# Decoder layer on one core: a fifth seven-product pair in the second feed-forward, and block sums made in the activation pool

## The chip, the cores and the metric

The kernel runs on one core of one Trainium2 chip. The metric is the time of one execution on the device, in microseconds (us), as the median of three runs. The engines are named as in the profile: PE multiplies matrices (PEld is its loading of stationary operands), DVE is VectorE, ACT is ScalarE, POOL is GpSimd, and SP is the queue that issues most loads.

## The reference

One decoder layer, in float32, for a sequence of 256 tokens of width 2048 with 16 learned tokens put ahead of it (272 rows in all):

```
s = concat(meta, x)
s = s + 0.5 * ffn(rms_norm(s), ffn1)             # silu(h Wg) * (h Wu), then Wd; inner width 5632
h = rms_norm(s)
q, k, v, b, c, u = split(h @ w_in)
y_att  = differential attention (8 heads, 2 softmaxes each, difference times lam), head norm
y_conv = b * shortconv(c * u)                    # 3 taps
s = s + (sum over both branches of sigmoid(h @ w_gate) * (y @ w_branch)) @ w_out
s = s + 0.5 * ffn(rms_norm(s), ffn2)
out = rms_norm(s)[16:]
```

The second feed-forward only has to be computed for the 256 real tokens. Its gate and up weights are 2048 x 11264, its down weights 5632 x 2048.

## The kernel before

**Products in two parts.** Every float32 operand is split into a high half, rounded for PE, and the rest, a low half. A product is the sum of three matmuls: high by high, low by high, high by low. For weights, ACT casts the loaded tile into `wh` (`cast`, line 503) and DVE subtracts to make `wl` (`rest`, line 506). There are three buffers of each (`W_BUFS`), and a buffer comes free when PE has read it last. Loaded weight tiles of 128 x 1024 lie in the tag `st`, with eight buffers (`raw_tile`, line 68).

**Stages.** The first feed-forward runs in two halves of its inner width with `linear` (line 311), in blocks of two chunks of weights; after each block it calls `store.tick()`. Then come the projections with attention and convolution between their blocks, the gates and branches (`Mixed`, line 510), the output projection (`Plain`, line 685), and the second feed-forward: three thirds of the inner width, of four, four and three gate-up linears, each third followed by two down linears, all of class `Mixed`.

**Direct and seven-product pairs.** `Mixed` treats two chunks of the contraction (256 rows) as a pair, with two halves of the tokens and two column groups of 512. A pair is thus a 2 x 2 by 2 x 2 product of blocks. A direct pair (kind D, line 565) does the eight block products, 24 matmuls of 128 x 512, in two slots. A seven-product pair (kind S, line 594) does seven, 21 matmuls, in four slots: `raw` (P1, C11), `sums` (P5, P7), `sums2` (P6, C21) and `single` (C12). It needs sums of weight blocks, `ta` (two blocks) and `tb` (two blocks), and sums of activation blocks. The sums of weights come from one of two places. Where `store.get` finds them, they are loaded from memory (lines 609, 626); elsewhere DVE makes them in four additions (lines 614, 615, 623, 624). The last down linear, u = 1 of the last third, takes every pair directly.

**The store.** The sums in memory are made early, from the raw weights, by `Store.tick` (line 281). Every `STEP` ticks a unit begins: it loads two tiles `ur` and `un` on SP; half a step later four additions on DVE make `ua` and `ub`, and POOL writes both to memory. All four tiles are `st` buffers. `store.want` lists the units in the order in which they are made, all but the third S pair of each linear.

**The order of the work.** `stream` (line 664) calls, for each slot n, the preparation of slot n + 2, the products of slot n, the steps placed after it, and then as many entries of the list `todo` as the slot's `room` says: two after the slots of a direct pair, none after those of a seven-product pair. `todo` holds DVE's combining of results (`Gated.late`, `Added.late`) and of the turned activations (`Pairs.turned`, placed after slots 4 and 5). DVE's operations in this part form a chain: they run in the order written. PE and ACT have no such chain; the scheduler that builds the program may put a later instruction of theirs ahead of one that would wait.

**Kinds and pools.** `HALF` gives the kinds of the eight pairs of the gate-up linears, `TURNED` with `ORDER` those of the down linears of the first two thirds, `SHORT` those of the last. An activation pair of kind D takes one slot of the pool `act` (`N_ACT` slots), one of kind S two. Small results lie in the tag `ev`, with eight buffers.

## Time and profile before

| | |
|---|---|
| median of three runs | 2189.27 us (2188.91 to 2189.32) |
| profiled execution, its own time | 2188.72 us |
| span of that execution, first to last instruction | 2186.9 us |
| granted clock of PE | 0.999 |
| PE busy | 2173.7 us, 99% of the span |
| DVE busy | 1643.5 us, 75% |
| ACT busy | 1109.3 us, 51% |
| moved by DMA | 542.09 MB, 248 GB/s on average |

The span is what the trace covers; the run's own time has 1.8 us around it. In the trace a line such as "L84 DVE TENSOR_TENSOR wl<-st,wh 128x1024" names the code line (a helper's, where one records every operation, as line 84 does for DVE and line 560 for PE), the engine, the operation, the tile written and the tiles read. A value in square brackets is the engine's idle time before the instruction, with what ended it. In rows of busy time by windows, each engine's busy us is followed by its number of instructions; the last three columns are the granted clock, the mean share of the DMA engines that were busy, and GB/s. The first feed-forward takes about the first 815 us, the projections with attention and convolution go to 1130, the gates and branches to 1388, the output projection to 1483, and the second feed-forward takes the rest.

### The profile page before, as it was taken

The numbers are of one execution on the slowest core, as the hardware profiler recorded it, in microseconds if no ns is written. First come the engines' busy times: TensorE is split into PE (matmuls) and PEld (weight loads), VectorE is DVE, ScalarE is ACT, GpSimd is POOL, SyncE is SP. The second block draws the span as 40 slices with busy tenths as digits, with TensorE's granted clock in tenths as the row PEclk, the third lists the DMA queues.
The fourth block names the chain that finished last, engine by engine and source line by source line (L and its number), as shares of the span: only waits on it lengthen the run. The fifth ranks groups of instructions, "written<-read, shape, count | busy, mean of one in ns | idle before, by whom it ended". The sixth has DMA issues, their size and how long they took to land.

```text
span 2186.9 us, 34858 instructions
## 1 busy us (share of the span) xinstructions
PE 2173.7 (99%) x13450; PEld 1955.7 (89%) x13450; DVE 1643.5 (75%) x2214; ACT 1109.3 (51%) x1431; POOL 60.6 (3%) x119
## 2 busy tenths in 40 slices
PE   9999999999999999999999999999999999999998
PEld 8999999999999999999988888888878888888886
DVE  7767665566766767666777787768888988888888
ACT  6434333333433444444445555556666566655665
POOL 0000000000000000000000000000000000000000
PEclk9999999999999999999999999999999999999999
DMA  7787888879888988744556665656777877878874
GB/s 238 263 309 275 294 295 288 301 261 317 302 276 287 320 294 303 260 145 135 167 162 212 212 207 190 211 180 216 250 239 258 280 238 259 273 244 277 282 244 154
DMA packets 240966, 542.09 MB, mean 248 GB/s; under 512 B 18564, under 2 KB 18624, under 8 KB 240800
## 3 DMA queue, kind: packets, MB, share of 16 engines
q1 hardware_dynamic: 225184, 484.25, 66.5%
q0 software_dynamic: 15232, 54.96, 6.7%
q8 instruction: 105, 1.72, 0.3%
q10 hardware_dynamic: 384, 0.66, 0.1%
q14 instruction: 61, 0.50, 0.1%
HBM read 486.18 MB, written 53.61 MB: 247 GB/s over the span
## 4 chain that ended last, share of the span: by engine, by line
PE 98%; ACT 1%; DVE 1%; DMA 1%; issue 0%; DVEq 0%
PE pgC L560 12%; PE pdC L560 7%; PE pgP L560 6%; PE gC L560 5%; PE pd L346 4%; PE pu L346 4%; PE pu L344 4%; PE pd L344 4%; PE pu L345 4%; PE pd L345 4%; PE pg L346 4%; PE pg L344 4%; PE pg L345 4%; PE zC L560 3%; PE o L709 3%; PE pgD L560 3%
## 5 line engine op out<-in xcount | busy, mean ns | idle before, releaser
L331 ACT CAST wh<-st 128x1024 fp32r<-128x1024 f32 x352 | 369.6, 1051 | 566.9 <-PE pd L345 134.8
L332 DVE TENSOR_TENSOR wl<-st,wh 128x1024 fp32r<-128x1024 f32 x352 | 429.6, 1222 | 273.8 <-ACT wh L331 273.2
L84 DVE TENSOR_TENSOR wl<-st,wh 128x1024 fp32r<-128x1024 f32 x246 | 299.3, 1220 | 85.2 <-ACT wh L504 78.2
L504 ACT CAST wh<-st 128x1024 fp32r<-128x1024 f32 x238 | 247.4, 1053 | 184.2 <-PE o L709 39.9
L344 PE MATMUL pg<-h,wh 128*128 128x272 f32 x704 | 202.8, 289 | 1.7 <-ACT wh L84 1.4
L344 PE MATMUL pu<-h,wh 128*128 128x272 f32 x704 | 203.2, 289 | 0.0
L346 PE MATMUL pd<-m,wl 128*128 128x272 f32 x704 | 203.0, 288 | 0.0
L346 PE MATMUL pu<-h,wl 128*128 128x272 f32 x704 | 203.0, 288 | 0.0
L344 PE MATMUL pd<-m,wh 128*128 128x272 f32 x704 | 203.0, 288 | 0.0
L345 PE MATMUL pu<-h,wh 128*128 128x272 f32 x704 | 202.4, 288 | 0.0
L345 PE MATMUL pd<-m,wh 128*128 128x272 f32 x704 | 202.4, 287 | 0.0
L345 PE MATMUL pg<-h,wh 128*128 128x272 f32 x704 | 201.4, 287 | 0.0
L346 PE MATMUL pg<-h,wl 128*128 128x272 f32 x704 | 199.7, 289 | 0.0
L560 PE MATMUL pgC<-wh,h 128*128 128x512 f32 x528 | 163.3, 391 | 0.0
L344 PEld LDWEIGHTS pg<-h,wh 128*128 128x128 f32 x704 | 132.3, 188 | 2.6 <-ACT wh L84 2.6
L504 ACT CAST wh<-ta 128x1024 fp32r<-128x1024 f32 x74 | 77.9, 1052 | 108.3 <-DVE ta L84 72.7
L345 PEld LDWEIGHTS pg<-h,wh 128*128 128x128 f32 x704 | 132.8, 189 | 0.0
L345 PEld LDWEIGHTS pu<-h,wh 128*128 128x128 f32 x704 | 132.7, 189 | 0.0
L345 PEld LDWEIGHTS pd<-m,wh 128*128 128x128 f32 x704 | 132.7, 189 | 0.0
L346 PEld LDWEIGHTS pu<-h,wl 128*128 128x128 f32 x704 | 132.5, 188 | 0.0
L346 PEld LDWEIGHTS pd<-m,wl 128*128 128x128 f32 x704 | 132.5, 188 | 0.0
L344 PEld LDWEIGHTS pu<-h,wh 128*128 128x128 f32 x704 | 132.2, 188 | 0.1
(479 smaller groups left out, 5162.0 us busy)
## 6 DMA issues: line engine op xcount, KB each, us to landing
st<-in_ffn_w_gu_dram SPq DMA_DIRECT2D x176, 512.0 KB, 5.9
st<-in_ffn_w_down_dram SPq DMA_DIRECT2D x140, 512.0 KB, 6.2
st<-in_w_in_dram SPq DMA_DIRECT2D x96, 512.0 KB, 4.4
st<-in_ffn_w_gu_dram SPq DMA_DIRECT2D x176, 256.0 KB, 4.3
sr<-in_ffn_w_gu_dram SPq DMA_DIRECT2D x44, 512.0 KB, 4.2
st<-in_w_gate_dram SPq DMA_DIRECT2D x40, 512.0 KB, 4.7
ur<-in_ffn_w_gu_dram SPq DMA_DIRECT2D x33, 512.0 KB, 7.8
un<-in_ffn_w_gu_dram SPq DMA_DIRECT2D x33, 512.0 KB, 5.0
```

What stands on the lines that cost most here:

```text
L84: r = f(*a, **k)
L331: act_.copy(out=wh[:, :m, :], in_=sw)
L332: dve_.tensor_sub(wl[:, :m, :], sw, wh[:, :m, :].bitcast(F32))
L344: nc.tensor.matmul(a, wh[:, i, f], act.part(c, 0, t0, t1), start=first, stop=False)
L345: nc.tensor.matmul(a, wh[:, i, f], act.part(c, 1, t0, t1), start=False, stop=False)
L346: nc.tensor.matmul(a, wl[:, i, f], act.part(c, 0, t0, t1), start=False, stop=last)
L504: nc.scalar.copy(out=wt[0][:, : sw.shape[1], :], in_=sw)
L560: nc.tensor.matmul(ps[:, f0:f1], x, wt[:, f0:f1], start=count[n] == self.whole[n], stop=count[n] == 1)
L709: nc.tensor.matmul(a, wh[:, i, f], act.both(c, 0, SEQ), start=first, stop=False)
```

## The change

The kinds get a fifth S pair (`FIVE` for `HALF`, and `TURNED`, with its order) and the last third's down linear a third one (`SHORT`). In the new order all S pairs of a linear stand together behind the direct ones. In linears with five S pairs the third one still makes its own sums; where there are fewer than five, all are loaded. The store's list grows from 47 to 63 units. Until the end of the first feed-forward a unit begins every five ticks, its four tiles are slots of the activation pool, and its additions are divided over two ticks; from the projections on it goes on with six ticks and `st` buffers. The activation pool gets two slots more, and small tiles (constants of the start, norms, attention) move into `ev` buffers. Slots of S pairs with loaded sums have room for one entry of `todo`.

```diff
-N_ACT = 28
+N_ACT = 30
...
-HALF = "DDDSSDSS"
-TURNED = "DSDSDSDS"
-ORDER = (0, 2, 4, 1, 3, 6, 5, 7)
-SHORT = "DDDSDS"
-STEP = 6
+FIVE = "DDDSSSSS"
+TURNED = "DSDSDSSS"
+ORDER = (0, 2, 4, 1, 3, 5, 6, 7)
+SHORT = "DDDSSS"
+STEP = 5
...
-    grow = const.tile([DC, P], F32, name="grow")
+    grow = ev([DC, P], "grow")
...
-                self.ssq = tmp.tile([P, T], F32, tag="ssq", name="ssq")
-            sq = self.ssq if first else tmp.tile([P, T], F32, tag="sq", name="sq")
+                self.ssq = ev([P, T], "ssq")
+            sq = self.ssq if first else ev([P, T], "sq")
...
+        def tile(self, name):
+            if self.step == STEP:
+                return apool.tile([P, 2, GW], F32, tag="act", name=name)
+            return raw_tile(name)
+
         def tick(self):
-            n = self.count % STEP
+            n = self.count % self.step
...
-                self.v = [raw_tile(n) for n in ("ur", "un")]
+                self.v = [self.tile(n) for n in ("ur", "un")]
...
-            if n == STEP // 2 and self.v:
+            if n == 3 and self.v:
+                r, x = self.v
+                ta = self.tile("ua")
+                self.v.append(ta)
+                nc.vector.tensor_add(ta[:, 0, :], r[:, 0, :], x[:, 0, :])
+                nc.vector.tensor_add(ta[:, 1, :], x[:, 1, :], x[:, 0, :])
+                nc.gpsimd.dma_start(out=self.units[0][-1][0], in_=ta.rearrange("p c f -> p (c f)"))
+            if n == 4 and self.v:
                 kept = self.units.pop(0)[-1]
-                (r, x), self.v = self.v, None
-                ta, tb = raw_tile("ua"), raw_tile("ub")
-                added(nc.vector, r, x, ta, tb)
-                for tl, to in zip((ta, tb), kept):
-                    nc.gpsimd.dma_start(out=to, in_=tl.rearrange("p c f -> p (c f)"))
...
+                (r, x, ta), self.v = self.v, None
+                tb = self.tile("ub")
+                nc.vector.tensor_add(tb[:, 0, :], ta[:, 0, :], x[:, 1, :])
+                nc.vector.tensor_add(tb[:, 1, :], tb[:, 0, :], r[:, 1, :])
+                nc.gpsimd.dma_start(out=kept[1], in_=tb.rearrange("p c f -> p (c f)"))
+
+        def slower(self):
+            assert self.v is None
+            self.step, self.count = STEP + 1, 0
...
+            room = 0 if kept is None else 1
...
-                Slot(raw, lambda: p((1, "P1", "r", 0), (2, "C11", "r", 1)), 0),
+                Slot(raw, lambda: p((1, "P1", "r", 0), (2, "C11", "r", 1)), room),
...
-    def in_store(kinds, order):
-        at = [g for g in order if kinds[g] == "S"]
-        return [g for n, g in enumerate(at) if n != 2]
+    def want(kinds, order, *place):
+        at = [k for k in order if kinds[k] == "S"]
+        for n, k in enumerate(at):
+            if n != 2 or len(at) < 5:
+                store.want(place[0], (place[1] + 2 * k) * P, *place[2:])
...
+    while store.v:
+        store.tick()
+    store.slower()
     for g in range(2):
         linear(h2, allk, w_in, 0, W2 + g * GW, 0, T, "k", qk_evict(kT, g, 0, "k"))
...
-    h3 = Pairs("h3", HALF)
+    h3 = Pairs("h3", FIVE)
```

More of the change, by code (lines that the diff above doesn't have):

```diff
@@ L123, in decoder_layer @@
     NV = 2 * DC + 3 * NH + 1
-    vrows = const.tile([NV, P], F32, name="vrows")
+    vrows = ev([NV, P], "vrows")
     G_MIX, G_FFN2, G_CONV, G_SUB = 0, DC, 2 * DC, NV - 1
@@ L135, in decoder_layer @@
     nc.gpsimd.dma_start(out=vrows[G_SUB:NV, :], in_=t["subln"])
-    lamv = const.tile([P, 4, HD], F32, name="lamv")
+    lamv = ev([P, 4, HD], "lamv")
     for i, n in enumerate(("lambda_q1", "lambda_k1", "lambda_q2", "lambda_k2")):
@@ L171, in make_lam @@
     def make_lam():
-        lprod = tmp.tile([P, 2, HD], F32, tag="lprod", bufs=1, name="lprod")
+        lprod = ev([P, 2, HD], "lprod")
         nc.vector.tensor_mul(lprod, lamv[:, 0:4:2, :], lamv[:, 1:4:2, :])
@@ L237, in end @@
             nc.tensor.matmul(ps[:, n0:T], ones, self.ssq[:, n0:], start=True, stop=True)
-            ms = tmp.tile([P, T], F32, tag="ms", bufs=1, name="ms")
+            ms = ev([P, T], "ms")
             nc.vector.tensor_scalar(ms[:, n0:], ps[:, n0:T], 1.0 / D, EPS, op0=ALU.mult, op1=ALU.add)
@@ L255, in rsqrt @@
     def rsqrt(out_, ms, shape, name):
-        a = tmp.tile([P, T], F32, tag="rsa", bufs=1, name="rsa" + name)[:, : shape[1]]
+        a = ev([P, T], "rsa" + name)[:, : shape[1]]
         nc.scalar.activation(a, ms, AF.Sqrt)
@@ L270, in __init__ @@
         def __init__(self):
-            self.units, self.kept, self.count, self.v = [], {}, -DC // KB, None
+            self.units, self.kept, self.count, self.v, self.step = [], {}, -DC // KB, None, STEP
         def want(self, w, r0, c0, c1):
@@ L644, in mixed @@
             self.slots += [
-                Slot(raw, lambda: p((1, "P1", "r", 0), (2, "C11", "r", 1)), 0),
-                Slot(sums, lambda: p((5, "P5", "a", 0), (4, "P7", "a", 1)), 0),
-                Slot(sums2, lambda: p((6, "P6", "b", 0), (3, "C21", "b", 1)), 0),
-                Slot(single, lambda: p((7, "C12", "s", 0)), 0),
+                Slot(raw, lambda: p((1, "P1", "r", 0), (2, "C11", "r", 1)), room),
+                Slot(sums, lambda: p((5, "P5", "a", 0), (4, "P7", "a", 1)), room),
+                Slot(sums2, lambda: p((6, "P6", "b", 0), (3, "C21", "b", 1)), room),
+                Slot(single, lambda: p((7, "C12", "s", 0)), room),
             ]
@@ L975, in decoder_layer @@
         for g in third:
-            for k in in_store(HALF, range(8)):
-                store.want(w_gu, 2 * k * P, g * GW, F + g * GW)
+            want(FIVE, range(DC // 2), w_gu, 0, g * GW, F + g * GW)
         kinds, order = (TURNED, ORDER) if whole else (SHORT, range(6))
         for u in range(2 if whole else 1):
-            for k in in_store(kinds, order):
-                store.want(w_down, (third[0] * GC + 2 * k) * P, u * W2, u * W2 + GW)
+            want(kinds, order, w_down, third[0] * GC, u * W2, u * W2 + GW)
     before1 = First()
@@ L1117, in values @@
             nc.vector.tensor_copy(oN[g][:, qt, j, :], po[:, :P])
-            junk = tmp.tile([P, P], F32, tag="junk", bufs=1, name="junk")
+            junk = ev([P, P], "junk")
             nc.scalar.activation(junk, oN[g][:, qt, j, :], AF.Square, accum_out=osq[:, qt, h : h + 1])
@@ L1395, in decoder_layer @@
             turns = []
+    assert not store.units
     stream(linears)
```

5 lines of the change are left out of this document (removed).

## The prediction

> **What bounds the kernel now.** I read the page first, then the busy time in chosen windows, then the timelines of three engines over one gate-up linear of the second feed-forward.
>
> ```profile
> span 2186.9 us, 34858 instructions
> ...
> PE 2173.7 (99%) x13450; PEld 1955.7 (89%) x13450; DVE 1643.5 (75%) x2214; ACT 1109.3 (51%) x1431; POOL 60.6 (3%) x119
> ...
> DMA  7787888879888988744556665656777877878874
> ...
> PE 98%; ACT 1%; DVE 1%; DMA 1%; issue 0%; DVEq 0%
> ...
> L560 PE MATMUL pgC<-wh,h 128*128 128x512 f32 x528 | 163.3, 391 | 0.0
> ```
>
> PE sets the end nearly alone. But 391 ns is the life of one matmul, and matmuls overlap; what one saves is the distance between starts. The first gate-up linear of the second third shows it: 180 matmuls lie between these two rows.
>
> ```profile
> 1736.48 0.62 PE L560 MATMUL pgC<-wh,h 128*128 128x512 f32 x2
> ...
> 1777.34 0.61 PE L560 MATMUL pgC<-wh,h 128*128 128x512 f32 x2
> ```
>
> 40.86 / 180 = 0.227 us each. The next rows cut a later linear (first third) into its stretches: three direct pairs, two seven-product pairs, one direct pair, two seven-product pairs; then three other places.
>
> ```profile
> 1567.56:1585.54 17.98, 17.98 (x85) 14.80 (x84) 16.11 (x20) 9.40 (x12) 0.00 (x0) 1.00 0.83 280
> 1585.54:1595.56 10.02, 10.02 (x46) 7.70 (x44) 8.12 (x11) 8.39 (x11) 0.00 (x0) 1.00 0.54 162
> 1601.02:1610.77 9.75, 9.75 (x43) 7.75 (x42) 8.15 (x9) 7.80 (x10) 0.00 (x0) 1.00 0.81 257
> 1567.56:1610.77 43.21, 43.21 (x193) 34.75 (x192) 37.80 (x46) 27.70 (x34) 0.00 (x0) 1.00 0.76 253
> ...
> 1610.00:1617.00 7.00, 7.00 (x33) 5.77 (x32) 6.88 (x10) 3.91 (x5) 0.00 (x0) 1.00 1.04 395
> ...
> 68.00:309.00 241.00, 241.00 (x1922) 241.00 (x1921) 164.35 (x223) 96.27 (x110) 13.82 (x26) 1.00 0.85 292
> ...
> 972.00:1130.00 158.00, 158.00 (x1159) 145.97 (x1158) 111.02 (x220) 72.39 (x136) 0.00 (x0) 1.00 0.51 156
> ```
>
> Two seven-product pairs are 42 matmuls, 9.52 us at 0.227; they take 10.02 and 9.75, so PE already loses 0.50 and 0.23 us there. The waits of the weight loads from 1480 us on name whom for:
>
> ```profile
> PEld pgP L560 <- DVE wl L84: 4.8, 15, 0.4
> PEld pgC L560 <- DVE wl L84: 2.1, 7, 0.3
> PEld pdP L560 <- DVE wl L84: 1.8, 6, 0.4
> PEld pdC L560 <- DVE wl L84: 0.9, 3, 0.3
> ```
>
> It is VectorE, late with the low half wl. So this stage has PE as its bound and DVE (37.80 of 43.21 us, 87%) just behind it, in runs of seven-product pairs above all.
>
> **What is taken away.** A direct pair is 24 matmuls, a seven-product pair 21. Eleven gate-up linears and five of the six down linears (the last stays all direct) turn one pair each: 16 x 3 = 48 matmuls, 48 x 0.227 = **10.9 us** off PE. By the means of the groups it would be 18.8; that would be an error.
>
> The Trainium skill (TensorE: Matmul & The Clock Gate, section "Wait — 56ns, not 53.3ns?") gives 215.7 ns between starts at 512 columns, which would make 10.4 us; its section "Back-to-back issue gap" has about 131 ns in a stream, which would make 6.3. The rows above agree with neither, and decide.
>
> **What the longer run costs.** Before, a linear goes D D D S S D S S; after, D D D S S S S S, 105 matmuls or 23.8 us in one run. Four of the five load their sums; the third (place 2) makes them itself, in four additions. Before, that pair stood behind a direct pair; now it stands behind two seven-product pairs. VectorE takes its work in the order written (a chain): rest of sr, two additions for ta, two for tb, rest of ta. The rows of VectorE and ScalarE for a self-made pair and for a loaded one behind another:
>
> ```profile
> 1596.99 1.22 DVE L84 TENSOR_TENSOR wl<-sr,wh 128x1024 fp32r<-128x1024 f32 x1
> 1598.12 0.68 DVE L84 TENSOR_TENSOR ta<-sr,sx 128x512 f32<-128x512 f32 x1
> 1598.72 0.68 DVE L84 TENSOR_TENSOR ta<-sx 128x512 f32<-128x512 f32 x1
> ...
> 1604.80 1.22 DVE L84 TENSOR_TENSOR wl<-sr,wh 128x1024 fp32r<-128x1024 f32 x1 [0.44 <-ACT wh L504]
> 1606.16 1.23 DVE L84 TENSOR_TENSOR wl<-ta,wh 128x1024 fp32r<-128x1024 f32 x1
> ```
> ```profile
> 1599.52 1.06 ACT L504 CAST wh<-ta 128x1024 fp32r<-128x1024 f32 x1 [2.90 <-DVE ta L84]
> ...
> 1603.71 1.06 ACT L504 CAST wh<-sr 128x1024 fp32r<-128x1024 f32 x1 [0.69 <-PE pgP L560]
> ```
> ```profile
> 1607.14 0.62 PE L560 MATMUL pgP<-wh,h3b 128*128 128x512 f32 x2
> ```
>
> Starts on DVE are 1.13 us apart behind a 1024-wide operation and 0.60 behind a 512-wide one. In a run the cast of sr cannot begin earlier than 1603.71: it waits for PE to give back one of three buffers. So a run leaves VectorE no lead, however early the data are. Put a self-made pair in the place of the loaded one: rest of sr from 1604.80, additions 1605.93 and 1606.53, ta there at 1607.21, cast done 1608.3. PE wants it at 1607.14: **1.2 us late**. Filling: PE may take the two first products of the last slot meanwhile, and the low half of ta is late behind the tb additions (1607.13 to 1608.33, rest done 1609.55, wanted 0.45 after the high half at 1608.75), 0.8 more. I take 1.25 a linear; bounds 0 (all filled) and 2.0.
>
> That holds where VectorE enters the run with nothing left over: first linears of the three thirds, second down linears of two, and the second gate-up of the last third, whose turned pairs are both direct: six. In the other linears the turned activations hold it up at the first pair:
>
> ```profile
> 1587.37 0.69 DVE L84 TENSOR_TENSOR ma<-xf,ma 128x512 fp32r<-128x512 f32 x1 [2.05 <-ACT ma L447]
> 1587.98 1.07 DVE L84 TENSOR_TENSOR xf<-xf 128x256 f32<-128x256 f32 x3
> 1588.97 1.22 DVE L84 TENSOR_TENSOR wl<-tb,wh 128x1024 fp32r<-128x1024 f32 x1
> ...
> 1594.72 2.35 DVE L84 TENSOR_TENSOR wl<-st,wh 128x1024 fp32r<-128x1024 f32 x2
> ```
>
> From 1588.97 it has no gap until the second pair is done at 1594.72, where now a direct pair gives it time (5.46 us of PE for two rests). After the change the next work there is the step the new pops bring forward (mb, 0.60), rest of sr (1.13), ta (1.28 to its landing), cast (1.1): 1598.8. PE, without loss, would want ta at 1585.54 + 0.09 (transposes) + 48 x 0.227 = 1596.5. Late by 2.3. Such a linear loses 0.5 today (0.09 of 0.50 is the transposes), some of which stays: **+2.0** each; bounds 0.1 (VectorE's work from 1588.97 to the run's last wl is 1.13 + 1.2 + 12.0 + 6.4 = 20.7, with 3 x 1.13 + 0.60 = 4.0 a loaded pair and 2.4 more a self-made one, ending 1609.7, PE's 1609.4, and no order of matmuls beats that) and 2.6. There are seven gate-up linears of this kind. The first down linears of two thirds now have two turned seven-product pairs ahead instead of one: one xf group and one 512 more, 0.99 + 0.60 on DVE, less what is hidden: +3.0 each (0.1 to 3.6). The down linear of the last third has a run of three, all loaded, behind such turns: +1.0 (-0.5 to 2).
>
> Sum: 6 x 1.25 + 7 x 2.0 + 2 x 3.0 + 1.0 = 28.5; less 10.9: **+17.6**. All low ends: -10.5; all high ends: +28.5.
>
> **What moves early on.**
>
> ```profile
> L303 DVE TENSOR_TENSOR ua<-un 128x512 f32<-128x512 f32 x47 | 32.2, 684 | 0.0
> ```
> ```profile
> SPq L325 <- DVE ub L304: 186.4, 46, 8.5
> ```
> ```profile
> sr<-in_ffn_w_gu_dram SPq DMA_DIRECT2D x44, 512.0 KB, 4.2
> ...
> sx<-in_ffn_w_gu_dram SPq DMA_DIRECT2D x33, 256.0 KB, 4.3
> ...
> ta<-sums0a SPq DMA_DIRECT2D x1, 512.0 KB, 3.2
> tb<-sums0b SPq DMA_DIRECT2D x1, 512.0 KB, 3.3
> ```
>
> 47 units become 63 (11 x 4 + 4 x 4 + 3). The first feed-forward gives 248 ticks of 241 / 80 = 3.01 us: 42 units at six ticks, 50 at five; the rest, 5 before and 13 after, go into the projections. A unit reads and writes 2.1 MB. Per tick 0.524 + 2.1/5 = 0.94 MB, 313 GB/s; the window shows 292 at a share of 0.85, so full is 343 and the share becomes 0.91. It stays under PE, and the weights have their eight buffers to themselves, where SP now waits 186 us for those the store holds: **0**. Its loads now wait on SP, ahead of weights, for a free activation slot; stream, h1 and m hold 4 + 8 + 12 = 24 of 30 and the store at most 5, and should one be late the eight weight buffers cover 24 us. If the bandwidth went, say 300 GB/s, a tick would take 3.14 us: +32. DVE gets 3.2 more units of four 0.60 us additions in those 241 us, beside 164: hidden. In the projections eight more units are 19 us on DVE, which is busy 111 of 158: hidden, at most 2. Constants and norms that go to the eight ev slots are used where PE has other work: 0.
>
> **The rivals.** (1) *The order hides it: faster.* PE's instructions aren't chained, and today it already runs later first-half products ahead of a late wl: the four waits above come to 9.6 us of weight loads, and cost 0.2 to 0.3 us a boundary. If that fills the new runs too, it is the low end: 2189.3 - 10.5 = **2178.8**. It decides where a linear loses less than 10.9 / 16 = 0.68 more. Against it: the late thing is here a high half, on which P5 and P7 whole hang. (2) *Even*: half of the stalls filled, 14 - 10.9: about 2192. (3) *Transfers set the run: slower still.* A loaded pair moves 1.84 MB, a self-made one 1.05; a run 8.4 MB in 23.8 us, 352 GB/s. By 253 / 0.76 = 333 it takes 25.2, +1.4 in 15 linears: 21 more, **2228**. Against it: the eight buffers hold 4 MB ahead, and one window had 395. (4) *The early stage is full*: +32, **2239**; against it the shares above.
>
> The Trainium skill (DMA: Bandwidth & Descriptors, section "Specifications") puts HBM at about 358 GB/s for a core, by which the run would have 6 GB/s to spare. The window of 395 GB/s is above that, so the trace doesn't agree.
>
> **How the numbers follow.** The sum stands against the profiled execution's own 2188.72 us (span 2186.9 and 1.8 around it): 2206.3. The median is 0.55 higher: **2206.9, say 2207**. Chances: forecast 0.60, (1) 0.17, (2) 0.10, (3) 0.08, (4) 0.05. A measurement here tells 0.2%, 4.4 us, from no change: faster is (1), 0.17; same (2), 0.10; slower the rest, 0.73. The range goes from 2183, which leaves out most of (1), to 2224, which holds the high ends (2218), 2 us of the projections and a part of (3). The forecast's own is 2194 to 2218.
>
> **What would show it.** Right: a clean gate-up linear takes 41.4 instead of 40.9 us, one with turns some 1.3 more than before; PE's losses stand at P5 of pair 5, "<- ACT wh" with "DVE ta" behind it; VectorE has no gap from the first pair to the fifth. Wrong: linears of 40.2 to 41.7 us, gaps on VectorE inside the run, a run whose idle times end on DMAs, or a matmul pitch over 3.01 us a tick in the first feed-forward.

## The result, and the profile after

The changed kernel takes 2270.9 us (median of four runs, 2268.4 to 2281.7) against 2189.2 before: a ratio of 1.038, 95% interval 1.035 to 1.042. The forecast was 2207, at most 2224. The sign was right, and the size was not: 82 us lost where 18 were expected.

The page of the changed kernel, its busy times, its DMA shares by slice, its chain and two groups of instructions:

```profile
span 2269.7 us, 35203 instructions
...
PE 2199.3 (97%) x13402; PEld 1955.3 (86%) x13402; DVE 1708.5 (75%) x2325; ACT 1141.2 (50%) x1474; POOL 77.9 (3%) x151
...
DMA  7888988977988988877666665557677778768874
...
PE 61%; issue 29%; DVE 5%; POOL 2%; ACT 1%; DMA 1%; POOLq 0%; DVEq 0%; SPq 0%; ACTq 0%
...
L356 PE MATMUL pd<-m,wl 128*128 128x272 f32 x704 | 205.8, 292 | 19.4 <-DVE wl L342 19.3
```

PE has 48 matmuls fewer (13402 for 13450), as the change says. The chain that ends last, 98% PE before, leaves PE for 39% of the span. In the first feed-forward PE now stands 19.3 us for VectorE's wl in the down products alone.

Where the time went is read from the first matmul of a stage. Before (timeline of PE):

```profile
815.42 0.29 PE L344 MATMUL k<-h,wh 128*128 128x272 f32 x1
...
1129.98 0.63 PE L560 MATMUL gC<-wh,h 128*128 128x512 f32 x2
...
1483.33 0.63 PE L560 MATMUL pgC<-wh,h 128*128 128x512 f32 x2
```

and after:

```profile
857.99 0.29 PE L354 MATMUL k<-h,wh 128*128 128x272 f32 x1
...
1176.16 0.63 PE L570 MATMUL gC<-wh,h 128*128 128x512 f32 x2
...
1529.41 0.63 PE L570 MATMUL pgC<-wh,h 128*128 128x512 f32 x2
```

The projections begin 42.6 us later, the gates 46.2, the second feed-forward 46.1. From there to the end of the span it was 703.6 us and is 740.3: 36.7 more. Two losses, then: **46 us early on**, where the prediction had 0, and **37 in the second feed-forward**, where it had 17.6.

**The early loss.** Which DMA VectorE waited for, and four windows of the first feed-forward (columns as in the prediction; the last three are granted clock, DMA share, GB/s):

```profile
DVE ua L302 <- DMA un<-in_ffn_w_gu_dram: 67.7, 20, 8.3
...
DVE ua L302 <- DMA un<-in_ffn_w_down_dram: 50.4, 12, 7.1
```
```profile
68.00:190.00 122.00, 121.72 (x968) 121.32 (x966) 81.40 (x112) 49.07 (x55) 8.58 (x16) 1.00 0.89 303
319.00:487.00 168.00, 150.10 (x1155) 147.88 (x1154) 95.12 (x119) 51.52 (x50) 13.87 (x26) 0.98 0.89 308
390.00:450.00 60.00, 50.30 (x390) 48.97 (x389) 34.47 (x45) 17.79 (x17) 5.88 (x11) 1.00 0.97 341
457.00:487.00 30.00, 28.70 (x229) 28.48 (x228) 16.25 (x17) 9.45 (x9) 1.07 (x2) 1.00 0.75 242
```

The first row comes near the rate that the prediction worked out (313 GB/s, share 0.91), and PE loses next to nothing in it. The second is the first down linear: 168 us for 1152 matmuls, which at the pitch of before's window (241.00 us for 1922) are 144.5. Of the 23.5 us lost there, 17.9 are idle time of PE; in the rest PE works more slowly (its granted clock is 0.98 in the mean; see below). Inside it lie 60 us at 341 GB/s and a share of 0.97, beside 30 us at 242. The average is as forecast; the traffic comes in bursts. In a burst the store's first addition of each unit stands between the weight blocks like this (timeline of VectorE):

```profile
403.38 0.69 DVE L302 TENSOR_TENSOR ua<-ur,un 128x512 f32<-128x512 f32 x1 [5.60 <-DMA un<-in_ffn_w_down_dram]
...
405.20 1.22 DVE L342 TENSOR_TENSOR wl<-st,wh 128x1024 fp32r<-128x1024 f32 x1
...
406.93 1.22 DVE L342 TENSOR_TENSOR wl<-st,wh 128x1024 fp32r<-128x1024 f32 x1
...
409.47 1.21 DVE L342 TENSOR_TENSOR wl<-st,wh 128x1024 fp32r<-128x1024 f32 x1
413.95 0.69 DVE L302 TENSOR_TENSOR ua<-ur,un 128x512 f32<-128x512 f32 x1 [3.27 <-DMA un<-in_ffn_w_gu_dram]
...
424.87 0.69 DVE L302 TENSOR_TENSOR ua<-ur,un 128x512 f32<-128x512 f32 x1 [5.02 <-DMA un<-in_ffn_w_gu_dram]
```
```profile
406.47 0.39 PE L356 MATMUL pd<-m,wl 128*128 128x272 f32 x1 [2.19 <-DVE wl L342]
```

In this stretch a unit comes every **three** weight blocks, not every five as the code says. (Elsewhere in the first feed-forward two to four units stand 2 to 5 blocks apart, and a pause of 8 to 11 blocks follows; behind this stretch it is 29.) Three blocks and a unit are 3 x 0.524 + 2.1 = 3.7 MB. At PE's own pace, three ticks of 3.01 us, they would need 406 GB/s; the transfers moved them in 10.6 us, 347 GB/s, at a share of 0.97. Each unit's load lands late, VectorE, which takes its work in order, stands 3 to 6 us at its addition, the next wl is late, and PE stands 2.19 us for it. The DMA queue is full of units that nobody needs before 1529 us.

**What a stall brings with it.** Three windows of 3.4 us, each right behind idle times of PE, in the first feed-forward, in the first k linear and in the first down linear of the second feed-forward, and PE at the beginning of the third:

```profile
194.40:197.80 3.40, 3.40 (x15) 3.40 (x16) 3.40 (x8) 1.39 (x3) 0.53 (x1) 0.50 0.92 293
866.80:870.20 3.40, 3.40 (x17) 3.40 (x16) 3.21 (x6) 1.52 (x3) 0.00 (x0) 0.50 1.05 416
1740.60:1744.00 3.40, 3.40 (x8) 2.72 (x9) 2.89 (x3) 1.90 (x3) 0.00 (x0) 0.51 0.96 271
```
```profile
1739.22 2.08 PE L570 MATMUL pdP<-wh,mb 128*128 128x512 f32 x5 [1.62 <-ACT wh L514]
1741.09 1.05 PE L570 MATMUL pdP<-wl,mb 128*128 128x512 f32 x2
```

The granted clock, the third number from the end, is 0.50 there, and in the third window eight matmuls take 3.4 us, 0.425 each instead of 0.227. Such stretches stand in the trace at 194, 369, 710, 867, 1741 and 2007 us, the second of 6.8 us and the others of 3.4; before has none ahead of its last 4 us. Together they are 23.9 us at half the clock, so that by estimate some 12 of the 82 us are this: about 7 in the first feed-forward, 1.5 in the first k linear, 3.4 in the second feed-forward. Each begins within 6 us of idle times of PE that come to 1.5 to 4.3 us; the stall of 1.63 us at pair 5 of a gate-up linear, shown next, has none behind it. At what idle time the clock falls was not measured.

**The second feed-forward.** One later gate-up linear of the second third, at its pair 5 (the self-made one). First PE, then VectorE, then ACT:

```profile
1868.67 0.40 PE L570 MATMUL pgC<-wl,h3a 128*128 128x512 f32 x1
1870.70 1.84 PE L570 MATMUL pgP<-wh,h3b 128*128 128x512 f32 x5 [1.63 <-ACT wh L514]
```
```profile
1867.07 1.22 DVE L84 TENSOR_TENSOR wl<-sr,wh 128x1024 fp32r<-128x1024 f32 x1
1868.20 0.68 DVE L84 TENSOR_TENSOR ta<-sr,sx 128x512 f32<-128x512 f32 x1
1868.81 0.68 DVE L84 TENSOR_TENSOR ta<-sx 128x512 f32<-128x512 f32 x1
```
```profile
1869.60 1.04 ACT L514 CAST wh<-ta 128x1024 fp32r<-128x1024 f32 x1 [3.05 <-DVE ta L84]
```

This is the chain that the prediction drew: rest of sr, two additions, ta, cast, P5; PE wants P5 0.23 us after 1868.67 and gets it at 1870.70, 1.8 us late. In a linear without turned activations the same place reads:

```profile
1824.55 0.39 PE L570 MATMUL pgC<-wl,h3a 128*128 128x512 f32 x1
1826.04 1.84 PE L570 MATMUL pgP<-wh,h3b 128*128 128x512 f32 x5 [1.10 <-ACT wh L514]
```

1.26 us late, where 1.2 was worked out.

Times of a linear, from its first matmul to the next linear's, in us. "Price" is after, less before without 3 x 0.227:

| linear | before | after | price | predicted |
|---|---|---|---|---|
| without turned activations (six) | 40.85 typical | 42.6 | 2.45 | 1.25 |
| later gate-up, with turned ones (seven) | 42.4 | 44.7 | 2.95 | 2.0 |
| first down linear of two thirds (1.7 of it at half the clock) | 42.4 | 46.9 | 5.1 | 3.0 |
| down linear of the last third | 32.6 | 33.1 | 1.1 | 1.0 |
| all seventeen | 694.9 | 730.6 | 46.6 | 28.5 |

The last linear, all direct, takes 32.6 us in both and stands only in the sum. The seventeen linears gain 10.9 us by their matmuls and pay 46.6.

### The profile page after: what moved, and what is told of

Read it like the earlier page. It is cut to its first block, busy times and chain, and to the rows that moved or that the text cites. A ratio compares the mean times of both kernels' runs of the same rounds, so it can differ in the third digit from the quotient of the medians.

```text
span 2269.7 us, 35203 instructions
## 1 busy us (share of the span) xinstructions
PE 2199.3 (97%) x13402; PEld 1955.3 (86%) x13402; DVE 1708.5 (75%) x2325; ACT 1141.2 (50%) x1474; POOL 77.9 (3%) x151
## 4 chain that ended last, share of the span: by engine, by line
PE 61%; issue 29%; DVE 5%; POOL 2%; ACT 1%; DMA 1%; POOLq 0%; DVEq 0%; SPq 0%; ACTq 0%
PE pgC L570 10%; PE pdC L570 6%; PE pgP L570 5%; PE gC L570 5%; PE zC L570 3%; PE o L720 3%; PE pdP L570 2%; DVE wl L84 2%; PE pgD L570 2%; PE pd L356 2%; PE pd L354 1%; PE pd L355 1%; PE gP L570 1%; PE o L721 1%; PE q L352 1%
## 5 line engine op out<-in xcount | busy, mean ns | idle before, releaser
L341 ACT CAST wh<-st 128x1024 fp32r<-128x1024 f32 x352 | 368.9, 1050 | 577.8 <-PE pd L355 139.0
L342 DVE TENSOR_TENSOR wl<-st,wh 128x1024 fp32r<-128x1024 f32 x352 | 428.0, 1221 | 200.1 <-ACT wh L341 187.0
L84 DVE TENSOR_TENSOR wl<-st,wh 128x1024 fp32r<-128x1024 f32 x214 | 261.1, 1220 | 77.3 <-ACT wh L514 70.4
L514 ACT CAST wh<-st 128x1024 fp32r<-128x1024 f32 x206 | 213.0, 1052 | 164.5 <-PE o L720 40.1
L356 PE MATMUL pd<-m,wl 128*128 128x272 f32 x704 | 205.8, 292 | 19.4 <-DVE wl L342 19.3
L356 PE MATMUL pu<-h,wl 128*128 128x272 f32 x704 | 205.1, 291 | 11.7 <-DVE wl L342 11.7
L356 PEld LDWEIGHTS pd<-m,wl 128*128 128x128 f32 x704 | 133.7, 190 | 22.4 <-DVE wl L342 22.2
L514 ACT CAST wh<-ta 128x1024 fp32r<-128x1024 f32 x90 | 94.6, 1051 | 114.4 <-DVE ta L84 62.6
L302 DVE TENSOR_TENSOR ua<-ur,un 128x512 f32<-128x512 f32 x63 | 43.4, 690 | 128.3 <-DMA un<-in_ffn_w_gu_dram 67.7
L84 DVE TENSOR_TENSOR wl<-tb,wh 128x1024 fp32r<-128x1024 f32 x90 | 110.0, 1222 | 34.9 <-PE pgP L570 15.2
L355 PEld LDWEIGHTS pd<-m,wh 128*128 128x128 f32 x704 | 133.9, 190 | 0.0
L354 PEld LDWEIGHTS pd<-m,wh 128*128 128x128 f32 x704 | 133.5, 190 | 0.0
```

Of the source, the lines that this page charges most:

```text
L84: r = f(*a, **k)
L302: nc.vector.tensor_add(ta[:, 0, :], r[:, 0, :], x[:, 0, :])
L341: act_.copy(out=wh[:, :m, :], in_=sw)
L342: dve_.tensor_sub(wl[:, :m, :], sw, wh[:, :m, :].bitcast(F32))
L354: nc.tensor.matmul(a, wh[:, i, f], act.part(c, 0, t0, t1), start=first, stop=False)
L355: nc.tensor.matmul(a, wh[:, i, f], act.part(c, 1, t0, t1), start=False, stop=False)
```

## The experiments

In the table the runs stand in the order in which they are told. The early column is the start of the gates less 1130.0, that of before; the last is the sum of the seventeen linears of the second feed-forward. Both are read from the one profiled execution of each kernel, which can lie some us off the median. By their matmuls alone, 48 fewer, these would take 694.9 - 10.9 = 684.0.

| kernel | median, us | ratio, 95% interval | early, us | linears, us |
|---|---|---|---|---|
| before | 2189.2 | | 0 | 694.9 |
| after | 2270.9 | 1.0349 to 1.0416 | +46.2 | 730.6 |
| early_alone | 2234.8 | 1.0194 to 1.0228 | +46.6 | 695.1 |
| paced | 2242.4 | 1.0226 to 1.0256 | +16.8 | 730.8 |
| in_st | 2244.4 | 1.0237 to 1.0268 | +22.2 | 730.7 |
| paced_first | 2212.5 | 1.0089 to 1.0119 | +19.6 | 698.6 |
| first | 2194.8 | 1.0016 to 1.0037 | +3.7 | 698.1 |
| hoist | 2220.7 | 1.0127 to 1.0161 | +1.8 | 724.4 |
| first_pool | 2212.0 | 1.0087 to 1.0117 | +2.6 | 715.8 |
| five_loaded | 2188.0 | 0.9986 to 1.0005 | +3.2 | 691.9 |
| loaded_split | 2182.7 | 0.9954 to 0.998 | +1.6 | 684.1 |
| split_second | 2215.7 | 1.0102 to 1.0136 | +3.3 | 719.2 |
| more_sums | 2190.3 | 0.9995 to 1.0013 | +0.3 | 690.0 |
| earlier_sums | 2190.5 | 1.0001 to 1.0019 | +6.1 | 689.9 |

### early_alone: the early part without the fifth pair

The kinds of before, with the third S pair self-made as before; the store's five ticks and its place in the activation pool stay.

```diff
-FIVE = "DDDSSSSS"
-TURNED = "DSDSDSSS"
-ORDER = (0, 2, 4, 1, 3, 5, 6, 7)
-SHORT = "DDDSSS"
+FIVE = "DDDSSDSS"
+TURNED = "DSDSDSDS"
+ORDER = (0, 2, 4, 1, 3, 6, 5, 7)
+SHORT = "DDDSDS"
...
-            room = 0 if kept is None else 1
+            room = 0
...
-            if n != 2 or len(at) < 5:
+            if n != 2:
```

> Kinds of the pairs, list of units and rooms as before (47 units); store, pools and ev buffers as after. Theory A (the units lost their pace: in the activation pool nothing holds them back, they come in bursts of one per 3 blocks, 3 x 0.524 + 2.1 = 3.7 MB per 9 us = 406 GB/s, more than the transfers carry, and VectorE waits in order for un): the early loss stands without the second feed-forward, 2189 + 46 = about 2235 us, projections beginning near 858 us. Theory B (the ev buffers or the end of the store cost the time): also about 2235, but with losses outside the bursts. If the loss came only with 63 units: about 2190.

Measured: 2234.8 us, 45.6 over before, with the second feed-forward's linears at 695.1, as before. So the two losses are separate: 81.7 less 45.6 leaves 36.1 for the second feed-forward, which has 36.7 in the profile. And the early one needs no longer list of units: 47 units made in the new way cost as much as 63 (46.6 us, all of it ahead of the projections, where these units are done).

### paced: the same units, held to the weight blocks

Each unit's loads are ordered behind the load of the weight block of their tick, and each pair of its additions behind that block's rest. Nothing else changes.

```diff
-                self.v = [self.tile(n) for n in ("ur", "un")]
-                for tl, cq in zip(self.v, (c0, c1)):
-                    nc.sync.dma_start(...)
+                self.v = [self.tile(n) for n in ("ur", "un")]
+                with after(load):
+                    for tl, cq in zip(self.v, (c0, c1)):
+                        nc.sync.dma_start(...)
...
+                with after(rest):
+                    nc.vector.tensor_add(ta[:, 0, :], r[:, 0, :], x[:, 0, :])
```

`after` tells the scheduler to put the instruction behind the given one in its order; no wait is written into the program for it.

> The kernel after, but each unit's loads stand behind the weights of their own tick on SP, and its additions behind wl of their own tick on VectorE, so that one unit comes every five blocks, 313 GB/s. Theory A: the early loss of 46 us goes, 2271 - 44 = about 2227 us, projections beginning near 816 to 820 us, the second feed-forward as in the kernel after (740 us). Rival (63 units at five ticks are simply more than the transfers carry, as the prediction's fourth rival had it): over 2255 us.

Measured: the projections begin at 815.9 us, 0.5 later than before. The first down linear in this kernel (window up to 463 us), and two units in VectorE's timeline:

```profile
319.00:463.00 144.00, 144.00 (x1149) 144.00 (x1148) 86.42 (x100) 50.11 (x48) 9.94 (x19) 1.00 0.91 318
815.90:1146.80 330.90, 321.15 (x2277) 292.67 (x2276) 237.19 (x438) 143.24 (x266) 14.94 (x28) 1.00 0.72 243
```
```profile
404.43 0.68 DVE L305 TENSOR_TENSOR ua<-ur,un 128x512 f32<-128x512 f32 x1
...
419.50 0.68 DVE L305 TENSOR_TENSOR ua<-ur,un 128x512 f32<-128x512 f32 x1
```

Units are 15.1 us apart, five ticks of 3.01, and VectorE doesn't wait at either. At 318 GB/s and a share of 0.91, the numbers of the prediction, PE isn't idle in those 144 us. This shows the early cause: not the amount, but that nothing tied the units to the weights. (Loads and additions were tied together; which of the two ties would do alone was not run.) The second row shows a price that I had not expected, and by which the total missed the expectation: in the projections, whose order isn't one of equal ticks, the same rule makes 318.2 us (after) into 330.9.

### in_st: the store back in the weights' buffers

The units keep five ticks and take `st` buffers again, as before; no pace is written.

```diff
         def tile(self, name):
-            if self.step == STEP:
-                return apool.tile([P, 2, GW], F32, tag="act", name=name)
             return raw_tile(name)
```

> The kernel after, but the units' tiles are st buffers all along, as in the kernel before, with five ticks. Theory A: st buffers are shared with the weights in order and so keep the pace; most of the early loss goes, 2225 to 2235 us. Rival (bandwidth at five ticks): over 2255 us. A third (half the st buffers are too few for five ticks): between, 2235 to 2255, with waits of PE for wh spread evenly.

Measured: the projections begin at 833.5 us, 18 late instead of 43. The total, 2244.4 us, lies in the range of the third theory, not of the first. Sharing the buffers with the weights does hold the units back: VectorE's first additions stand five blocks apart again (4 to 7, a few times 3). But VectorE waits for `un` as long as in after, 122.8 us in 42 places against 118.1 in 32, and PE loses less than half of what it loses there. So the sum of VectorE's waits doesn't measure PE's loss. Nor are these 18 us shown to be a part of after's 43: with the pool kept and only the pace written (paced), 0.5 is left. Why even units land late in `st` buffers was not settled.

### paced_first: the self-made pair at the head of the run

paced, with the first S pair of each linear made by VectorE instead of the third.

```diff
-            if n != 2 or len(at) < 5:
+            if n != 0 or len(at) < 5:
```

> As paced, but of five S pairs the first makes its own sums (it stands behind a direct pair) and the third is loaded. Theory C (the place: behind two seven-product pairs VectorE has no lead, and P5 waits for rest of sr, two additions and a cast): the second feed-forward loses about 1.8 us less in each of 15 linears, 27 us below paced, about 2200. Rival (VectorE's sum of work over the run is the bound, wherever the additions stand): less than 8 us below paced.

Measured: the linears fall from 730.8 to 698.6 us. 32 of the 36 us that they cost more than before come from the place of the one self-made pair (some 3 of them through the clock, which doesn't halve in these linears now). Behind a direct pair VectorE has time for four additions; behind two S pairs it hasn't.

### first: pace only where the ticks are equal

paced_first, with the pace kept only while the store is in the activation pool.

```diff
-            after = lambda r: nullcontext() if r is None else tc.issue_after(r.ins)
+            after = lambda r: nullcontext() if r is None or self.step != STEP else tc.issue_after(r.ins)
```

> As paced_first, but the pace is kept only while the units lie in the activation pool; in the projections they go as in the kernel after. Paced and paced_first took 331 and 334 us for the projections, the kernel after 318, the kernel before 315. Theory D (the fixed order of the additions behind wl hurts beside attention): 16 us below paced_first's 2212, about 2197 us. Rival (eight more units there cost it in any order): above 2207.

Measured: 2194.8 us, and the projections take 318.2 instead of the 334 of paced_first. What is left of them over before (3.6 us) lies in the two blocks of k, which come first: 28.6 us instead of 25.0, where the change drains the unit in hand before it slows the store. Here too the clock reads 0.50 for 3.4 us behind two idle times of 0.75; hoist and loaded_split drain in the same way, keep the clock, and take 27.1. So the drain itself is 2.1 us and the clock 1.5. The kernel is 0.3% slower than before (1.0016 to 1.0037): the linears still pay 14.1 us for their 10.9.

### hoist: the additions ahead of the rest

The third pair self-made again, but the two additions for ta stand ahead of the rest of sr, which PE wants later.

```diff
                 cast(v["r"], r)
-                rest(v["r"], r)
                 if kept is None:
                     dve.tensor_add(ta[:, 0, :], r[:, 0, :], x[:, 0, :])
                     dve.tensor_add(ta[:, 1, :], x[:, 1, :], x[:, 0, :])
+                rest(v["r"], r)
                 cast(v["a"], ta)
```

> Paced in the first feed-forward as in the run named first; the third S pair still makes its own sums, but its two additions for ta stand ahead of the rest of sr on VectorE, all else the same. Theory C (the lateness of P5 is the chain rest of sr, ta, cast): P5 is released 1.1 us sooner in 15 linears, the second feed-forward's linears fall from 730.8 by some 12 to 17 us, total about 2213. Rival (VectorE's total over the run): no change, 730, total 2227.

Measured: 724.4 us, only 6.4 less than paced: about 0.5 in each linear without turned activations, 1.6 in each first down linear, where the clock doesn't halve any more, and nothing in the later gate-up linears (44.7 as before the edit). PE in one of those:

```profile
1556.83 0.63 PE L574 MATMUL pgC<-wh,h3a 128*128 128x512 f32 x2
1558.26 0.50 PE L574 MATMUL pgP<-wh,h3b 128*128 128x512 f32 x1 [0.80 <-ACT wh L518]
...
1559.05 0.86 PE L574 MATMUL pgP<-wh,h3b 128*128 128x512 f32 x3
1560.72 0.50 PE L574 MATMUL pgP<-wh,h3b 128*128 128x512 f32 x1 [0.81 <-ACT wh L518]
```

Two stalls of 0.97 and 0.98 us have taken the place of one of 1.79. Where VectorE runs without a gap, an exchange of two of its operations moves the lateness and doesn't lessen it. The expectation that the order within the pair sets the price fell here.

### first_pool: GpSimd makes the additions

first, with the four additions of the self-made pair on GpSimd.

```diff
-                    dve.tensor_add(ta[:, 0, :], r[:, 0, :], x[:, 0, :])
+                    adder.tensor_add(ta[:, 0, :], r[:, 0, :], x[:, 0, :])
...
+            adder = nc.gpsimd if self.name.startswith("p") else dve
```

> As first, with the four additions of the self-made pair on GpSimd instead of VectorE. If VectorE's work in the run is what is left of the loss (paced_first: 698.6 us of linears against 694.9 before), the linears fall to 690 to 694 us and the total to about 2190. Rival (GpSimd is too slow for it, or slows VectorE's own operations beside it): no gain or a loss, 698 us and more, seen in a longer mean of VectorE's operations or in casts that wait for GpSimd.

Measured: 715.8 us, 17.7 more than first. GpSimd's additions and two groups of VectorE beside them:

```profile
L639 POOL TENSOR_TENSOR tb<-ta,sx 128x512 f32<-128x512 f32 x15 | 31.6, 2105 | 0.0
```
```profile
L84 DVE TENSOR_TENSOR wl<-st,wh 128x1024 fp32r<-128x1024 f32 x214 | 279.1, 1305 | 82.6 <-ACT wh L518 78.0 <-ACT wh L84 3.5
...
L84 DVE TENSOR_TENSOR q5d<-w,q5d 128x512 f32<-128x512 f32 x11 | 18.5, 1683 | 0.0
...
L84 DVE TENSOR_TENSOR u<-pgC,w 128x512 f32<-128x512 f32 x11 | 7.5, 680 | 0.0
```

and the first two of VectorE in first:

```profile
L84 DVE TENSOR_TENSOR wl<-st,wh 128x1024 fp32r<-128x1024 f32 x214 | 261.1, 1220 | 77.5 <-ACT wh L518 71.1 <-ACT wh L84 3.4
...
L84 DVE TENSOR_TENSOR q5d<-w,q5d 128x512 f32<-128x512 f32 x11 | 7.5, 685 | 0.0
```

An addition takes 1.7 to 2.1 us there instead of 0.69, and a VectorE operation that falls beside it up to 2.5 times as long, if it reads both inputs from on-chip memory (SBUF): q5d does. The operations u<-pgC,w, which read one input from PSUM, where PE writes its results, keep 680 ns, though ten of the eleven run beside an addition of GpSimd. The Trainium skill (GPSIMD Engine Reference, section "Specifications") says that GpSimd shares its way to the on-chip memory with VectorE and that they contend when VectorE's instruction has two inputs there; by the table of its section "Engine selection" an addition with two inputs is about half as fast on GpSimd. The trace agrees with the first, and shows 2.5 to 3 times for the second, with VectorE at work beside it.

### five_loaded: no self-made pair at all

In linears with five S pairs the third one loads the sums that belong to the second, so that nothing is made in place; the values computed are therefore not the layer's. It shows what the run of five costs without additions.

```diff
+            else:
+                key = lambda j: (place[0].tensor.name, (place[1] + 2 * j) * P, place[2])
+                store.kept[key(k)] = store.kept[key(at[n - 1])]
```

> Paced as in first; the third S pair's own additions are left out, it loads the sums of the second S pair in their place (so its products are of other weights). VectorE does 2.4 us less a linear, the transfers 0.8 MB more. Theory C: the linears of the second feed-forward fall from 730.8 to 688 to 692 us, below the 694.9 of the kernel before, total about 2188. Rival (transfers: 9.2 MB in a run of 23.8 us, 386 GB/s): 705 us or more, with waits for the loads.

Measured: 691.9 us, 38.7 less than after. Of the 46.6 us of the price, 38.7 are thus the additions with the stalls and the clock that follow them, and 7.9 the run of five itself. These 7.9 are spread unevenly: ten of the seventeen linears have 0.3 or less of it, one has 1.9. Such a run in one linear:

```profile
1550.00:1575.00 25.00, 24.65 (x104) 18.75 (x104) 22.64 (x26) 18.71 (x22) 0.00 (x0) 1.00 0.92 330
```

VectorE is busy 22.64 of 25 us and the transfers have a share of 0.92: both bounds that the prediction named for the run are close at once, and neither alone was shown to set the 7.9.

### loaded_split: a direct pair inside the run

five_loaded with the order D D S D S S S S, with the same sums of another pair.

```diff
-FIVE = "DDDSSSSS"
+FIVE = "DDSDSSSS"
...
-ORDER = (0, 2, 4, 1, 3, 5, 6, 7)
+ORDER = (0, 2, 1, 4, 3, 5, 6, 7)
```

> As five_loaded (the third S pair of five loads the sums of the second in place of making its own), but the order of the pairs is D D S D S S S S: a direct pair stands inside the run. Theory E (what is left of the loss after five_loaded, 691.9 us of linears with some 7 more of stalls than before, comes of a run in which VectorE needs 4.0 of each 4.76 us and gets no pause): the linears fall by 4 to 7 us, the total to about 2182. Rival (it comes of the hand-over at the end of a linear, or of the transfers): no change, 2188.

Measured: 684.1 us, 10.8 less than before, and 2182.7 in all (0.9954 to 0.998; the profiled execution was the fastest of five, 2179.4). That is as much as the 48 matmuls, 10.9 by the pitch of 0.227 us, but the two kernels differ in one thing more: before makes the third pair's sums itself and this one makes none. Four of the six linears without turned activations show the saving by itself, since PE hardly idles in them in either kernel: 40.8 to 40.9 us before, 40.1 to 40.4 here, where the pitch gives 0.68 less. With a direct pair between the first S pair and the other four, the run costs nothing over before, as long as all its sums are loaded.

### split_second: the same order, with its own sums

The order of loaded_split; VectorE makes the second S pair, behind the inner direct pair.

```diff
-            if n != 0 or len(at) < 5:
+            if n != 1 or len(at) < 5:
```

> A whole kernel with the 63 units: paced as in first, order D D S D S S S S, and the second S pair, behind the inner direct pair, makes its own sums. Theory E with C (a self-made pair costs nothing behind a direct one, and the break gives VectorE time): at or below first, 2188 to 2196 us. Rival (three loaded pairs right behind a self-made one find VectorE 2.4 us behind, wherever it stands): 2197 to 2205.

Measured: 2215.7 us, linears 719.2; the expectation missed. Four of the six linears without turned activations take 40.7 to 40.9 us, 0.6 over PE's own time: a direct pair ahead is enough there. With turned activations a gate-up linear takes 44.6, and the first down linears take 46.2 and 46.4, with the clock at 0.50 for 3.4 us in each. The slots of the inner direct pair have room for two entries of `todo` each, and VectorE's order shows what they hold: in one such linear it waits 2.5 us for ma, and makes ma, xf and mb between 1547.2 and 1551.7 us, ahead of the rest of sr and the additions. Below, the waits of PE's weight loads in the second feed-forward, of after, of first, and of more_sums (next); split_second's own are 27.7 us in 33 places:

```profile
PEld pgP L570 <- ACT wh L514: 36.6, 47, 2.1
```
```profile
PEld pgP L574 <- ACT wh L518: 8.2, 19, 0.5
```
```profile
PEld pgP L575 <- ACT wh L519: 3.1, 5, 0.9
```

### more_sums: own sums only where they cost little

The layer's values again. 73 units instead of 63; only five linears, all without turned activations, make their second S pair themselves. There is no drain at the start of the projections (which go on at six ticks), and the last eight units are made beside the branch and the output projection.

```diff
-            if n != 1 or len(at) < 5:
+            if n != 1 or not own:
...
-            want(FIVE, range(DC // 2), w_gu, 0, g * GW, F + g * GW)
+            want(FIVE, range(DC // 2), g == third[0], w_gu, 0, g * GW, F + g * GW)
...
-    while store.v:
-        store.tick()
-    store.slower()
+    store.mode(False, STEP + 1, (3, 4))
...
+    store.mode(False, 8, (5, 6))
+    for l in linears:
+        if isinstance(l, Plain) or l.name == "z":
+            for slot in l.slots:
+                slot.after.append(store.tick)
```

> The order of loaded_split (two direct pairs, a loaded one, the third direct one, four S pairs) with what it left out put back: 73 units instead of 63, all written before they are read. Only the linears with raw activations that follow one without turned activations (the first gate-up linear of each third, and the second down linear of the first two thirds) still make their second S pair themselves; every other linear loads four. Up to the projections a unit is made every five weight blocks with its place in the order fixed; through the projections every six; the seven units that are left are made beside the branch and the output projection, one for eight slots. Theory that the self-made pair costs most where VectorE also prepares turned activations or a first down linear: the second feed-forward falls from split_second's 719.2 us to some 686 (loaded_split showed 684.1 with all four loaded, and split_second 40.8 for a self-made second pair in the linears kept here), the stages up to the gates end within 4 us of before, so 2183 to 2187 us, under 2189. Rival: the ten further units cost beside the projections, the branch and the output projection (VectorE standing for a load, weights late) what the second feed-forward gains: 2189 or more, with that time found between 815 and 1483 us of the span.

Measured: 2190.3 us, no different from before (0.9995 to 1.0013). Before, then more_sums, from the projections to the second feed-forward:

```profile
815.40:1130.00 314.60, 314.60 (x2277) 291.46 (x2276) 218.78 (x404) 145.78 (x266) 5.85 (x11) 1.00 0.62 200
1130.00:1483.30 353.30, 353.02 (x1690) 294.23 (x1689) 268.01 (x328) 188.83 (x229) 2.12 (x4) 1.00 0.60 199
```
```profile
815.30:1130.30 315.00, 314.85 (x2277) 291.36 (x2276) 240.49 (x444) 145.47 (x266) 16.48 (x31) 1.00 0.79 267
1130.30:1489.40 359.10, 355.41 (x1690) 293.61 (x1689) 285.76 (x363) 189.71 (x233) 10.65 (x20) 1.00 0.70 238
```

The linears gain 4.9 us; the gates, the branch and the output projection take 5.8 more (1.8 the branch, 4.0 the output projection). The rival of the expectation was right.

### earlier_sums: the last units in the projections instead

more_sums with five ticks in the projections, so that four units are left for the branch and none for the output projection.

```diff
-    store.mode(False, STEP + 1, (3, 4))
+    store.mode(False, STEP, (3, 4))
...
+    while store.v:
+        store.tick()
+    store.n = 0
     store.mode(False, 8, (5, 6))
```

> more_sums with one change: through the projections a unit is made every five weight blocks instead of every six, so that four of the 73 are left for the branch and none for the output projection (more_sums made eight there, and took 4.0 us more than before in the output projection and 1.9 in the gates and the branch, while its projections took what they take in before). Theory that the units cost there because VectorE stands for their loads in a stretch that has little slack, and that the projections have room for four more: the projections stay within 1 us of before (314.6), the output projection is back at 94.8, the second feed-forward stays at 690, so 2184.5 to 2187.5 us, under 2189. Rival: the projections pay for the faster pace (a late weight block each, as they did for the drain of a unit in first), and the time is 2189 or more with the projections 3 us or more over 314.6.

Measured: 2190.5 us (1.0001 to 1.0019).

```profile
815.90:1136.10 320.20, 316.18 (x2277) 291.40 (x2276) 248.33 (x460) 144.91 (x266) 20.75 (x39) 1.00 0.84 283
```

From the gates to the second feed-forward it is 353.1 us, as before (353.3), so the four units in the branch cost nothing; the projections take 320.2 instead of 315.0. The rival holds again. The four units in the output projection cost 4.0 us and the four further ones in the projections 5.2, 1.0 to 1.3 us a unit, where the pair that a unit turns saves 3 x 0.227 = 0.68. No kernel with the layer's values was found that beats the one before. By estimate from these numbers one that leaves the four dear pairs direct would be some 2 us under it (4.9 less 4 x 0.68 and 0.3), 0.1%; it was not tried.

## Why the prediction was right or wrong

**What is taken away: right.** PE has 48 matmuls fewer, and a linear in which it hardly idles is 0.5 to 0.7 us shorter in loaded_split, for 3 x 0.227. That all its linears together come to 10.8 us is in part luck, since it leaves out additions that before makes.

**What moves early on: wrong, and the larger miss.** The step that failed is the **0** worked out from 313 GB/s and a share of 0.91. Those numbers are nearly what paced shows (318, 0.91), and at them PE loses nothing. But I took the five ticks of the code for the pace on the chip. Before, a unit's tiles were `st` buffers like the weights' own, handed out in the order written, so the unit couldn't come much before its place (in before, VectorE's additions for it stand 5 to 7 blocks apart, six in the code). In the activation pool nothing tied it to the weights; the program was built with units three blocks apart in stretches, and there the demand at PE's pace (406 GB/s) is more than the stretch moved (341). I wrote that the eight weight buffers would cover 24 us "should one be late", and looked only at what SP waits for. What stood was VectorE, whose order holds each wl behind the additions of a unit whose load had not landed: 118 us of waiting in 32 places (67.7 + 50.4). Not all of this reaches PE: it stood 31 us for wl in the first feed-forward (19.3 in the down products, 11.7 in the up products), and its clock was at 0.50 for 13.6 us there, some 7 us more by estimate. The rival "the early stage is full" had the place and nearly the size (+32), by a mechanism that wasn't the cause: the bandwidth didn't go, it was used too early. Of the 46.2 us, 42.6 are this; 3.6 are the drain in the blocks of k (28.6 us for 25.0; more_sums, without a drain, has 25.0), 1.5 of it through the clock, in a stage that I had at most 2 for. That a stall could cost the clock as well I had not thought of: every matmul was priced at the full clock. (The 3.2 further units that I counted in 241 us are 80/5 less 80/6, 2.7; nothing hangs on it.)

**What the longer run costs: right in place and mechanism, too small.** P5 of pair 5 is late behind ta, as drawn: 1.26 us for 1.2, and with turned activations 1.8 for 2.3. paced_first shows that the self-made pair's place is 32 us of it. The terms were mis-sized: 2.45 for 1.25, 2.95 for 2.0, 5.1 for 3.0, 1.1 for 1.0, together 46.6 for 28.5. Three things were missing. In the clean linear shown, the stall at P5 is followed by 0.5 us in the same pair, by 0.3 at the last pair of the run and by 0.2 where the next linear begins, 2.3 in all where before has none; I took PE to fill most of the late low halves with other products, and wrote 1.25 with 2.0 as the upper bound. The run of five costs 7.9 us even with every sum loaded, which I had at nothing beside the self-made pair: five_loaded has VectorE at 22.64 of 25 us and the transfers at 0.92 there. And in each of the two first down linears the stall takes the clock with it, 1.7 us.

**The rivals.** "The order hides it" fell: PE ran nothing in these stalls (1.10 and 1.63 us idle) while a whole first product was missing. "Transfers set the run" was priced at 21 us and may hold a part of the 7.9 us, which is all that a run without additions costs. "Slower" had 0.73 and was right; the range missed because the early loss alone is more than the 17 us that it left above the forecast, and the mis-sized terms add 18 on the same side.

**The signs.** A clean gate-up linear at 41.4: 42.6. One with turns 1.3 more than before: 2.3 more. Losses at P5 of pair 5 behind ACT's wh and VectorE's ta: shown. No gap of VectorE's from the first pair to the fifth: shown in the linear with turns (none from 1859.7 us to the fifth pair's rest of sr at 1878.2, and 0.36 there); in the clean one VectorE idles 0.46 just before the pair's rest of sr. A pitch over 3.01 us a tick in the first feed-forward was named as what would make the prediction wrong, and it did: 168.0 us for 48 blocks is 3.50.

## What to carry to other kernels

When background work is moved from a shared pool of buffers to one of its own, what is lost with the sharing is its pace: look at the order in which its instructions end up on each engine, not at the interval that the source gives, and tie it to the work that it runs beside. An average rate that fits says nothing of a burst that an in-order engine must wait through. A stall can cost more than its length: look at the granted clock right behind it. Of work that saves 0.68 us a piece, price the preparation of a piece in every stage that could hold it before adding more of it; here the stage with room took about 50 units, and the last ones, in the output projection and at a faster pace in the projections, cost 1.0 to 1.3 us each.

## What the runs showed of the hardware

Soon behind idle times of PE that come to 1.5 to 4.3 us, the granted clock falls to 0.50 for 3.4 us (once 6.8), and a 128 x 512 matmul takes 0.425 us instead of 0.227: six times in after, in before not until its last 4 us. Not every such stall has this behind it. GpSimd slows VectorE: beside 512-wide additions of 1.7 to 2.1 us on GpSimd, VectorE operations of 685 ns with both inputs in SBUF take 1683 in the mean, and those with one input from PSUM keep 680. And the transfers, reads and writes together, held 341 GB/s over 60 us at a share of 0.97; with PE never idle they held 318 at 0.91 over 144 us (paced). The 395 of the prediction was a window of 7 us. The Trainium skill (DMA: Bandwidth & Descriptors, section "Specifications") has about 358 GB/s of HBM for a core; the 60 us agree with that, the short window doesn't.
